# Storing one tile of a fused matmul in nine row pieces, and the tiles after it in six transfers

## The chip, the cores and the metric

One core of a Trainium2 chip. The metric is the device time of one execution in microseconds (us). Most executions of one kernel agree within 0.3%. Ratios are the mean time of one kernel's runs over that of the other's of the same rounds on the same chip, so they are not quite the ratio of the medians that are quoted; brackets give a 95% interval. A difference of 2% is the line for "faster" or "slower".

## The reference

```python
x: [16, 512, 1024] f32   weight: [1024, 768] f32   bias: [768]   residual: [16, 512, 768] f32
return (np.matmul(x, weight) + bias + residual).astype(np.float32)
```

The 8192 rows are worked in 64 tiles of 128 rows. 25.2 MB are written and 61.9 MB read.

## The kernel before

Each tile is cast to bf16, transposed and multiplied on TensorE (PE), and added to its residual on VectorE. All loads and stores are issued by SyncE (its queue is "SPq" in the profile), strictly in the order of one list, each, as the code reads, as soon as what it needs is finished (`# ...` marks what is cut; the comments are mine):

```python
ORDER = [ # ... kind, group S of 16 tiles, first and last tile in it, cuts in the 128 rows
 ('r', 3, 7, 16), ('s', 2, 0, 16), ('s', 3, 0, 10), ('s', 3, 10, 11, 104), ('s', 3, 11, 13),
 ('s', 3, 13, 14), ('s', 3, 14, 15), ('c', 3, 15, 0), ('c', 3, 15, 1)]
# ...
    def pump():
        while queue:
            kind, S, j0, j1, *cut = queue[0]
            # ...
            else:
                need = [("out", J * S + j) for j in range(j0, j1)]
            if not all(n in done for n in need):
                return                      # the head of the list holds up all the rest
            queue.pop(0)
            # ...
                edges = [0, *cut, P]
                for p0, p1 in zip(edges, edges[1:]):
                    K_(nc.sync.dma_start(
                        out=out_d[S, p0:p1, j0:j1, n0:n0 + nl],
                        in_=R[p0:p1, (J * S + j0) % RR:(J * S + j0) % RR + j1 - j0, n0:n0 + nl],
                    ))
```

So `('s', 2, 0, 16)` stores tiles 32 to 47 in one transfer, `('s', 3, 0, 10)` tiles 48 to 57, and `('s', 3, 10, 11, 104)` tile 58 as 104 and 24 rows. The semaphore (a counter that tells when all of a transfer has landed, that is, been written) is not in the code: the framework gives it out.

Of the kernel before, what the change touches and what calls it, by code (L numbers as in the profile page):

```python
# [32 lines left out]
 ('r', 0, 6, 16), ('x', 0, 14, 16), ('x', 1, 0, 6), ('r', 1, 0, 6), ('x', 1, 6, 16),  # L33
 ('r', 1, 6, 16), ('s', 0, 0, 16), ('x', 2, 0, 6), ('r', 2, 0, 6), ('x', 2, 6, 16),
 ('r', 2, 6, 16), ('s', 1, 0, 16), ('x', 3, 0, 6), ('r', 3, 0, 7), ('x', 3, 6, 16),
 ('r', 3, 7, 16), ('s', 2, 0, 16), ('s', 3, 0, 10), ('s', 3, 10, 11, 104), ('s', 3, 11, 13),
 ('s', 3, 13, 14), ('s', 3, 14, 15), ('c', 3, 15, 0), ('c', 3, 15, 1)]
LAST = [(0, 512), (512, 256)]


# [256 lines left out]
```

## Time and profile before

| | before |
|---|---|
| time, median | 210.32 us |
| span of the profiled run (that run took 210.12 us) | 208.3 us |
| PE busy | 201.8 us, 97% |
| DMA, 16 engines, main queue | 98.1% |
| last compute instruction ends | 204.5 us |
| last store issued, landed | 204.54, 207.25 us |

Both PE and DMA are nearly always busy.

### The profile page before, as it was taken

To read this page: it belongs to the slowest core of one execution; us is meant where nothing else is said; L and a number is where in the kernel's file an instruction comes from. 1 tells how busy PE (TensorE), PEld (TensorE's weight loads), DVE (VectorE), ACT (ScalarE), POOL (GpSimd) and SP (SyncE) were. 2 spreads that over 40 slices of the span, in tenths; PEclk is the share of its full clock that TensorE was granted. 3 is DMA by queue.
4 is the path that set the end of the run, shared out by engine and by line. 5 is a ranking of instruction groups with operands and counts; after the bars stand their busy time and mean duration, and the time that the engine had idled before them with its cause. 6 is when DMAs were issued, how large, how long until landed. Compare 5 with 4: busy or idle time off the path is not lost.

```text
span 208.3 us, 3115 instructions
## 1 busy us (share of the span) xinstructions
PE 201.8 (97%) x1298; PEld 130.1 (62%) x1298; DVE 104.7 (50%) x140; ACT 66.1 (32%) x69; POOL 116.0 (56%) x72
## 2 busy tenths in 40 slices
PE   7899999999999999999999999999999999999991
PEld 2455666666666666666666666666666666666651
DVE  0457555445545544654554454555445545544542
ACT  2444513403640272420370094230092046430000
POOL 2100029759999905999029702999207950599500
PEclk9999999999999999999999999999999999999998
DMA  6999999999989999999999999999999999999995
GB/s 233 427 429 436 424 432 457 388 446 421 495 383 466 405 423 427 434 426 415 425 465 418 422 436 452 415 437 406 434 446 451 409 419 475 428 396 444 416 368 221
DMA packets 4927, 87.24 MB, mean 419 GB/s; under 512 B 557, under 2 KB 685, under 8 KB 1841
## 3 DMA queue, kind: packets, MB, share of 16 engines
q1 hardware_dynamic: 4913, 87.05, 98.1%
q8 instruction: 10, 0.16, 0.3%
q14 instruction: 4, 0.03, 0.0%
HBM read 61.88 MB, written 25.17 MB: 418 GB/s over the span
## 4 chain that ended last, share of the span: by engine, by line
PE 92%; DMA 4%; DVE 1%; SPq 0%; ACT 0%; issue 0%
PE psum_o L164 78%; PE pt L157 13%; DMA x_tile<-in_x_dram 4%; PE psum_o L258 1%; DVE xt L158 0%; ACT xb L146 0%; DVE ro L262 0%; SPq L119 0%; SPq L122 0%
## 5 line engine op out<-in xcount | busy, mean ns | idle before, releaser
L164 PE MATMUL psum_o<-w_sb,xt 128*128 128x512 bf16 x1008 | 174.0, 326 | 0.5 <-DVE xt L158 0.3
L164 PEld LDWEIGHTS <-xt 128*128 128x128 bf16 x1008 | 98.5, 98 | 59.2 <-DVE xt L158 0.7
L189 POOL TENSOR_TENSOR ro<-ro,bias_sb 128x768 f32<-128x768 f32 x50 | 88.9, 1823 | 48.2 <-DMA ro<-in_residual_dram 37.7
L149 ACT CAST xb<-x_tile 128x1024 bf16<-128x1024 f32 x60 | 59.7, 1043 | 113.9 <-DMA x_tile<-in_x_dram 74.1
L158 DVE COPY xt<-pt 128x1024 bf16<-128x1024 bf16 x64 | 44.1, 691 | 84.4 <-PE pt L157 84.4
L199 DVE TENSOR_TENSOR ro<-psum_o,ro 128x768 f32<-128x768 f32 x49 | 46.5, 948 | 4.6 <-POOL ro L189 3.4
L185 POOL TENSOR_TENSOR ro<-ro 128x768 f32<-128x768 f32 x14 | 25.0, 1820 | 25.0 <-DMA ro<-in_residual_dram 25.0
L157 PE MATMUL pt<-ident,xb 128*128 128x128 f32 x256 | 38.3, 273 | 0.6 <-DVE xb L149 0.4
L157 PEld LDWEIGHTS pt<-ident,xb 128*128 128x128 f32 x256 | 29.7, 140 | 9.0 <-ACT xb L146 1.1
L195 DVE TENSOR_TENSOR ro<-psum_o,bias_sb 128x768 f32<-128x768 f32 x14 | 13.2, 947 | 0.0
L208 PE MATMUL psum_o<-warm 128*128 128x512 bf16 x12 | 4.8, 587 | 1.2 <-DVE warm_a L204 1.2
L229 ACT CAST w_sb<-ro 128x768 bf16<-128x768 f32 x4 | 3.3, 832 | 3.7 <-DMA ro<-in_weight_dram 3.7
L208 PEld LDWEIGHTS <-warm 128*128 128x128 bf16 x12 | 1.6, 141 | 3.9 <-issue 2.7
L229 POOL CAST w_sb<-ro 128x768 bf16<-128x768 f32 x1 | 0.8, 824 | 5.5 <-DMA ro<-in_weight_dram 5.5
L149 DVE CAST xb<-x_tile 128x1024 bf16<-128x1024 f32 x1 | 0.7, 694 | 4.5 <-DMA x_tile<-in_x_dram 4.5
L146 ACT CAST xb<-x_tile 128x512 bf16<-128x512 f32 x3 | 1.8, 617 | 3.4 <-PE psum_o L164 1.7
L258 PE MATMUL psum_o<-w_sb,xt 128*128 128x512 bf16 (+1 forms) x16 | 2.8, 326 | 0.0
L229 DVE CAST w_sb<-ro 128x768 bf16<-128x768 f32 x3 | 1.7, 556 | 2.0 <-DMA ro<-in_weight_dram 2.0
L147 DVE CAST xb<-x_tile 128x512 bf16<-128x512 f32 x3 | 1.2, 424 | 2.6 <-DMA x_tile<-in_x_dram 2.6
L258 PEld LDWEIGHTS <-xt 128*128 128x128 bf16 x16 | 1.6, 98 | 1.1
L223 PE MATMUL psum_o<-warm 128*128 128x512 bf16 x6 | 1.6, 379 | 0.0
L262 DVE TENSOR_TENSOR ro<-psum_o,ro 128x512 f32<-128x512 f32 (+1 forms) x2 | 1.1, 557 | 0.9 <-PE psum_o L258 0.8
(14 smaller groups left out, 5.1 us busy)
## 6 DMA issues: line engine op xcount, KB each, us to landing
out_dram<-ro SPq DMA_DIRECT2D x3, 6144.0 KB, 34.1
x_tile<-in_x_dram SPq DMA_DIRECT2D x3, 5120.0 KB, 24.1
ro<-in_residual_dram SPq DMA_DIRECT2D x3, 3840.0 KB, 25.3
x_tile<-in_x_dram SPq DMA_DIRECT2D x3, 3072.0 KB, 40.2
ro<-in_residual_dram SPq DMA_DIRECT2D x3, 2304.0 KB, 17.5
x_tile<-in_x_dram SPq DMA_DIRECT2D x4, 1024.0 KB, 8.3
x_tile<-in_x_dram SPq DMA_DIRECT2D x2, 2048.0 KB, 21.0
out_dram<-ro SPq DMA_DIRECT2D x1, 3840.0 KB
```

The costliest lines, as they stand in the source:

```text
L146: K_(nc.scalar.copy(out=dst[:, 0:K // 2], in_=src[:, 0:K // 2]))
L149: K_((nc.scalar.copy if how == "s" else nc.vector.tensor_copy)(out=dst, in_=src))
L157: K_(nc.tensor.transpose(out=pt[:, q, :], in_=words[:, ts(q, P)], identity=ident))
L158: K_(nc.vector.tensor_copy(out=XT[t % XT_N].rearrange("p q m e -> p (q m e)"), in_=pt.rearrange("p q m -> p (q m)").bitcast(BF16),))
L164: K_(nc.tensor.matmul(PO[t % HEAD][:, n0:n0 + nl], lhsT=XT[t % XT_N][:, q, :, e], rhs=w_sb[:, q, e, n0:n0 + nl], start=(q == 0 and e == 0) ...
L185: K_(nc.gpsimd.tensor_add(out=r, in0=r, in1=tmp(t)))
L189: K_(nc.gpsimd.tensor_add(out=r, in0=r, in1=bias_sb))
L195: K_(nc.vector.tensor_add(out=tmp(t), in0=p, in1=bias_sb))
L199: K_(nc.vector.tensor_add(out=row(t), in0=p, in1=row(t)))
L208: K_(nc.tensor.matmul(PO[0][:, 0:512], lhsT=warm[:, 0:P], rhs=warm, start=True, stop=True))
L229: K_(copy(out=w_sb[:, q, e, :], in_=w_st[:, 2 * q + e, :]))
L258: K_(nc.tensor.matmul(p, lhsT=XT[t % XT_N][:, q, :, e], rhs=w_sb[:, q, e, n0:n0 + nl], start=(q == 0 and e == 0), stop=(q == n_q - 1 and e ...
```

## The change

The intent is balance. The 16 DMA engines don't end together (the parts of the last store land from 206.18 to 207.25 us), and a transfer of few rows goes to some of the engines only: the prediction says to which, and from which page that is. The change gives tile 48 to the engines unevenly, and tile 58 evenly, together with 59 and 60:

```diff
- ('r', 3, 7, 16), ('s', 2, 0, 16), ('s', 3, 0, 10), ('s', 3, 10, 11, 104), ('s', 3, 11, 13),
- ('s', 3, 13, 14), ('s', 3, 14, 15), ('c', 3, 15, 0), ('c', 3, 15, 1)]
+ ('r', 3, 7, 16), ('s', 2, 0, 16), ('s', 3, 0, 1, 8, 15, 21, 26, 30, 33, 35, 126),
+ ('s', 3, 1, 10), ('s', 3, 10, 13), ('s', 3, 13, 14), ('s', 3, 14, 15), ('c', 3, 15, 0),
+ ('c', 3, 15, 1)]
```

## The prediction

> **What bounds the kernel now.** I read the page first, then the windows, then the DMA queue's own timeline and waits, and last the single packet and landing records of the trace.
>
> The page offers two candidates: PE is busy 97% of the span, the main DMA queue 98.1%.
>
> ```profile
> PE 201.8 (97%) x1298; PEld 130.1 (62%) x1298; DVE 104.7 (50%) x140; ACT 66.1 (32%) x69; POOL 116.0 (56%) x72
> ...
> q1 hardware_dynamic: 4913, 87.05, 98.1%
> q8 instruction: 10, 0.16, 0.3%
> ```
>
> Both run nearly without a gap, so the end decides. The windows (columns: busy us and count of each engine, then PE clock, DMA share, GB/s) show it:
>
> ```profile
> 180.00:206.00 26.00, 24.05 (x158) 15.51 (x156) 12.96 (x17) 3.14 (x3) 15.35 (x9) 1.00 0.97 407
> ...
> 204.00:205.00 1.00, 0.05 (x1) 0.00 (x0) 0.42 (x1) 0.00 (x0) 0.00 (x0) 1.00 0.87 350
> 205.00:206.00 1.00, 0.00 (x0) 0.00 (x0) 0.00 (x0) 0.00 (x0) 0.00 (x0) 1.00 0.97 368
> 206.00:207.00 1.00, 0.00 (x0) 0.00 (x0) 0.00 (x0) 0.00 (x0) 0.00 (x0) 0.91 0.28 99
> ```
>
> Compute is over at 204.5 us, and DMA still works at 0.97 until 206. The last store (256 columns of tile 63) is issued at 204.54. Its sixteen landing records lie between 206.18 and 207.25; the span ends at 208.3. The engines with no backlog needed 1.64 us (206.18 - 204.54); the slowest were 1.1 us late. So the DMA engines, not PE, set the end, and only by that 1.1 us. But they have no slack: any time in which they stand empty in the last 20 us is added to the end almost whole, because all of tiles 48 to 63 (6.29 MB) has still to be stored.
>
> The DMA queue's timeline at the end (start us, duration us):
>
> ```profile
> 157.96 0.34 SPq L130 DMA_DIRECT2D out_dram<-ro  x1
> ...
> 188.32 0.34 SPq L130 DMA_DIRECT2D out_dram<-ro  x1
> ...
> 191.36 1.64 SPq L130 DMA_DIRECT2D out_dram<-ro  x2
> ...
> 197.44 0.36 SPq L130 DMA_DIRECT2D out_dram<-ro  x1
> ```
>
> At 157.96 tiles 32 to 47 go out; at 188.32 tiles 48 to 57, the moment tile 57 is finished; then 58 in two, 59 and 60, and the rest. The first of these takes long to land, as the issues in 157 to 160 us show (KB, us to landing):
>
> ```profile
> out_dram<-ro SPq DMA_DIRECT2D x1, 6144.0 KB, 35.6
> ```
>
> 157.96 + 35.6 = 193.5. Its sixteen parts land one by one from 189.98 to 193.53; the rings go on with tiles 48 to 57 without a gap, because those were queued at 188.32, five microseconds before that last landing.
>
> One more thing bounds issues. The trace names the semaphore of each DMA, and the 36 of them go strictly round eight: 101, 104, 105, 106, 107, 108, 109, 110, 101 and so on. A DMA waits for the earlier one of its semaphore to land wholly. The ninth (x rows 6 to 9) and the tenth (residual) need no data of anyone, yet wait, as the queue's waits in 4.5 to 8 us say:
>
> ```profile
> SPq L124 <- DMA ro<-in_weight_dram: 1.5, 1, 1.5
> SPq L122 <- DMA x_tile<-in_x_dram: 0.6, 1, 0.6
> ```
>
> They start at 5.60 and 7.48; the first and second DMA landed at 5.58 and 7.47. At the end of before the rule costs nothing: the last eight stores use 107 to 106, and the last waits (at 204.39) for semaphore 106, which is that of tiles 32 to 47 and landed at 193.53.
>
> **What the Trainium skill says.** "DMA: Bandwidth & Descriptors", section "Why a DMA increments its semaphore by 16 and not by 1", says that a transfer is cut over the largest k up to 16 that divides its rows, on the lowest-numbered engines, and that only the full count means landed. The trace agrees: with k = 13 for 104 rows and 12 for 24, the packets I expect are exactly the 4913 of the page. So 8, 7, 6, 5, 4, 3, 2, 91 and 2 rows go to 8, 7, 6, 5, 4, 3, 2, 13 and 2 engines. The page's "Rules for kernel authors" ask for one semaphore per DMA; here eight are shared and guarded by waits. "Runtime: NRT & Kernel Launch", section "Instruction fetch mechanics", says instructions come in 16 KiB blocks: the 10 packets of q8 are these, some 19.5 us apart, at 177.13 and 196.13 last. It calls them mostly hidden for the sequencer; for a DMA engine they are not: the two engines hit last finish tiles 48 to 57 at 202.56 and 202.59, the next at 201.22, and eight 30,720-byte packets with a fetch took 10.57 us instead of 9.08, so 1.49 us each.
>
> **The change part by part.** The intent reads plainly: engines 0 and 1 get 15 rows of tile 48, falling to 7 for engines 8 to 12 and none for 13 to 15, and tile 58 goes back to 8 each. Per engine against before (18 rows for 0 to 11, 16 for 12, 8 for 13 to 15) that is +5 rows for engines 0 and 1, -3 for 8 to 11, 0 for 13 to 15. A row of 3072 bytes took 0.12 us, so this shifts at most 0.6 us. The two latest engines in before sent no packet of tile 58, so they are among 13 to 15 and gain nothing. From balance I expect 0.
>
> The issues are the larger matter. The S=3 stores become 15, numbers 28 to 42 counted from 0, with semaphores 107, 108, 109, 110, 101, 104, 105, 106, 107, 108 and so on. Tile 48 is ready at about 188.3 - 9 x 3.04 = 160.9 us.
> - Numbers 28 to 32 (8 to 4 rows): predecessors landed by 157.2; issued at once.
> - 33 (3 rows, 104): waits for the x load that landed at 169.34.
> - 34 (2 rows, 105): waits for the residual that landed at 179.23.
> - 35 (91 rows, 106): its predecessor is the store of tiles 32 to 47, so it waits until 193.53.
> - 37 (tiles 49 to 57), ready at 188.3, stands behind it in the same queue.
>
> So the issue of 3.5 MB moves from 188.32 to: 193.55, plus 0.41 for the 91 rows, plus 0.4 to 1.25 for the 2 rows (0.35 and 1.24 are the two short issues of before), so 194.4 to 195.2. From issue to first packet the last two stores took 0.83 and 0.95 us; I take 0.9 to 1.1. The engines, which ran out of tiles 32 to 47 between 189.5 and 193.1, restart on tiles 49 to 57 at 195.3 to 196.3.
>
> From there nothing waits for compute any more, and an engine needs, with the packet steps of before (bytes: us) 27,648: 1.024; 3072: 0.118; 2048: 0.081; 1024: 0.043, and 9216: 0.345 between 6144 and 16,384:
> 8 x 1.024 = 8.20; 8 x 0.345 = 2.76; two tiles of 8 x 0.118 = 1.88; 0.65; 0.34; in all 13.86 us with the small closing packets. Landing came 0.37 us after the last packet. An undisturbed engine lands at 195.8 + 13.86 + 0.37 = 210.0, that is 2.8 us later than 207.25.
>
> The engine that gets PE's fetch at 196.1 has 1.0 to 1.5 us more. PE's instructions don't change, so the fetch comes at the same time, now on an engine that has no spared tile ahead of it. Landing 211.0 to 211.7: +3.8 to +4.5 us. The other parts (seven more issues, their waits, one transfer for 58 to 60 at the same 197.44) lie beside this. With the middle, +4.0: 210.32 + 4.0 = 214.3.
>
> **The rivals.** (1) Balance works and nothing else happens: 209.6 to 210.4. For it speaks the 1.1 us of lateness; against it that the latest engines are not relieved, and the round of eight. (2) The stores of tile 48 fill time while the others wait, the restart is early and the fetch costs only 0.5 us: landing at 195.4 + 13.86 + 0.37 + 0.5 = 210.1, so 213.2. (3) Short transfers are slow to issue: if each of the two that stand before number 37 takes 1.24 us, it is issued at 196.1, restarts the engines at 197.1, lands at 211.3 without the fetch, and the time is 214.4 to 215.2. (4) PE as the bound: no store of the end is awaited by compute, so PE should not move.
>
> **Range and chances.** If the wait for semaphore 106 appears, 212.9 to 215.2 covers the spread of issue cost and fetch; I give that nine chances in ten. The 2% line is 214.53, inside this range and just above my middle, so slower by over 2% is nearly even. Nothing can make it faster by 2%, which would be 4.2 us of at most 0.7 to be had.
>
> **What would show it.** In the profile of after: the queue's waits should have an L130 entry for its own stores' DMA, with the 91-row store and that of tiles 49 to 57 issued after 193.5; DMA share near 0 around 194; PE's end unchanged at 204.1; the final wait of the queue (2.4 us before) some 4 us longer. I am wrong if tiles 49 to 57 are issued at 188.3 again: then the semaphores are given out otherwise, and rival 1 holds.

## More of the kernel before

What counts is the tail of the span: after the last compute instruction only stores are left. The prediction shows the lines for this; three windows that it doesn't show are needed later (columns: stretch in us, its length, busy us and number of instructions of PE, PEld, DVE, ACT and POOL, clock granted to PE, DMA share, GB/s):

```profile
190.00:192.00 2.00, 2.00 (x14) 1.18 (x13) 1.33 (x2) 0.00 (x0) 2.00 (x3) 1.00 0.74 316
192.00:194.00 2.00, 2.00 (x16) 1.40 (x14) 1.18 (x2) 0.00 (x0) 2.00 (x2) 1.00 1.03 445
194.00:196.00 2.00, 2.00 (x16) 1.36 (x15) 0.52 (x2) 0.00 (x0) 1.35 (x1) 1.00 0.96 415
```

A packet is counted in the stretch in which it starts, so single windows swing; the last two say that the engines were full between 192 and 196 us.

## The result, and the profile after

213.44 us (213.44 and 213.45 in two runs) against 210.32: ratio 1.0148 [1.0105, 1.0192]. It is slower by 1.5%, under the 2% line and inside the range. A second visit gave 213.53 against 210.61, ratio 1.0134 [1.0120, 1.0148].

The page of after (part 1, then the main queue of part 3) shows the same work, in 211.4 us:

```profile
PE 202.4 (96%) x1298; PEld 130.2 (62%) x1298; DVE 104.6 (49%) x140; ACT 66.1 (31%) x69; POOL 115.9 (55%) x72
...
q1 hardware_dynamic: 4938, 87.05, 96.8%
```

There are 25 more DMA packets for the same 87.05 MB, and a share that fell by 1.3 points. The windows say when it fell:

```profile
190.00:192.00 2.00, 2.00 (x14) 1.17 (x12) 1.32 (x2) 0.00 (x0) 2.00 (x2) 1.00 0.24 97
192.00:194.00 2.00, 2.00 (x16) 1.41 (x14) 1.20 (x2) 0.00 (x0) 2.00 (x2) 1.00 0.05 8
194.00:196.00 2.00, 2.00 (x16) 1.35 (x15) 0.52 (x2) 0.00 (x0) 1.24 (x1) 1.00 0.93 335
```

Between 192 and 194 us the engines moved 8 GB/s where they had moved 445, while PE worked as before; the 8 are one fetched block of PE's instructions (16 KiB, at 193.03), and no row of a store was begun. The queue's timeline tells why (start us, duration us):

```profile
157.80 0.34 SPq L131 DMA_DIRECT2D out_dram<-ro  x1
...
160.84 1.67 SPq L131 DMA_DIRECT2D out_dram<-ro  x5
...
193.67 0.31 SPq L131 DMA_DIRECT2D out_dram<-ro  x1
...
194.03 0.26 SPq L131 DMA_DIRECT2D out_dram<-ro  x1
...
194.38 0.36 SPq L131 DMA_DIRECT2D out_dram<-ro  x1
```

Five pieces of tile 48 go out at once, the sixth and seventh at 169.67 and 179.13. Then the queue stops: the piece of 91 rows is issued at 193.67, the last two rows at 194.03, and tiles 49 to 57 only at 194.38, where before had issued tiles 48 to 57 at 188.32. What it waited for, in 185 us to the end (us in total, times, longest):

```profile
SPq L131 <- DMA out_dram<-ro: 14.3, 1, 14.3
...
SPq L293 <- DMA out_dram<-ro: 4.7, 1, 4.7
```

The first line is the new one: 14.3 us for an earlier store. In the trace's instruction record, the 91-row issue waits on semaphore 106, which it also takes itself; that is the semaphore of the store of tiles 32 to 47, whose last landing record is at 193.65, 0.02 us before the issue. The second line is the wait at the kernel's end, 2.4 us in before. The chain of work still ends in the same place, as its last piece shows in before and after in turn (start us, us):

```profile
204.09 0.42 DVE ro L262
```

```profile
204.08 0.42 DVE ro L263
```

So compute did not move at all. The last landing did, from 207.25 to 210.34 us, 3.09 us later, and this is the whole loss (210.32 to 213.44 is 3.12).

### The profile page after: what moved, and what is told of

It reads as the page before. It is cut to its first block, busy times and chain, and to the rows that moved or that the text cites. A ratio compares the mean times of both kernels' runs of the same rounds, so it can differ in the third digit from the quotient of the medians.

```text
span 211.4 us, 3125 instructions
## 1 busy us (share of the span) xinstructions
PE 202.4 (96%) x1298; PEld 130.2 (62%) x1298; DVE 104.6 (49%) x140; ACT 66.1 (31%) x69; POOL 115.9 (55%) x72
## 3 DMA queue, kind: packets, MB, share of 16 engines
q1 hardware_dynamic: 4938, 87.05, 96.8%
## 4 chain that ended last, share of the span: by engine, by line
PE 91%; DMA 4%; DVE 1%; SPq 0%; ACT 0%; issue 0%
PE psum_o L165 77%; PE pt L158 13%; DMA x_tile<-in_x_dram 4%; PE psum_o L259 1%; DVE xt L159 0%; ACT xb L147 0%; DVE ro L263 0%; SPq L120 0%; SPq L123 0%
## 5 line engine op out<-in xcount | busy, mean ns | idle before, releaser
L209 PE MATMUL psum_o<-warm 128*128 128x512 bf16 x12 | 5.3, 632 | 1.2 <-DVE warm_a L205 1.2
L224 PE MATMUL psum_o<-warm 128*128 128x512 bf16 x6 | 1.6, 379 | 0.0
```

The source lines that it names most:

```text
L209: K_(nc.tensor.matmul(PO[0][:, 0:512], lhsT=warm[:, 0:P], rhs=warm, start=True, stop=True))
```

## The experiments

The theory: eight semaphores are given out in turn, and each transfer waits for the landing of the one eight before it. Nine pieces put the 91-row piece eighth after the long store of tiles 32 to 47, and tiles 49 to 57 stand behind it in an ordered queue. The rivals: that uneven rows on few engines, or the number of issues (15 instead of 8), or moving tile 48 ahead, cost the time themselves.

### Six pieces

```diff
-('s', 3, 0, 1, 8, 15, 21, 26, 30, 33, 35, 126)
+('s', 3, 0, 1, 8, 15, 21, 26, 37)
```

> Tile 48 in six transfers (8, 7, 6, 5, 11, 91 rows) instead of nine, all else as in the changed kernel. Theory (the eighth transfer after the store of tiles 32 to 47 takes its semaphore and waits for its landing): the eighth is now the store of tiles 58 to 60, which isn't ready before 197.4, so tiles 49 to 57 are issued at 188.3 and nothing is lost: 210.2 to 210.6 us. Rival A (uneven rows, or transfers on fewer than 16 engines, cost the time themselves): rows are about as uneven as in the changed kernel, 212.5 to 213.5. Rival B (each further issue costs): a proportional part, 212.2. Last instruction fetch of PE: near 196 as in the kernel before, since the DMA engines stay busy.

Measured: 210.82 us against 210.53, ratio 1.0012 [0.9996, 1.0029]. The median is 0.22 us above the expected band; the bands of these runs were worked out from 210.32 for the kernel before, which itself took 0.21 more here. The ratio is that of an equal. Tiles 49 to 57 went out as soon as they were ready:

```profile
188.77 0.35 SPq L131 DMA_DIRECT2D out_dram<-ro  x1
```

The queue still waited once for an earlier store, for 5.3 us, but now with the store of tiles 58 to 60, which was then not ready before 197.9 anyway. PE's last instruction fetch began at 197.84 us.

### Seven pieces

```diff
-('s', 3, 0, 1, 8, 15, 21, 26, 30, 33, 35, 126)
+('s', 3, 0, 1, 8, 15, 21, 26, 30, 37)
```

> Tile 48 in seven transfers (8, 7, 6, 5, 4, 7, 91 rows), one more than in the run of six. Theory: the eighth transfer is the store of tiles 49 to 57 itself; it is issued at about 193.7 instead of 188.3, first packets 194.6 to 194.7, then 13.86 us of packets and 0.37 to land: 208.9, so 211.8 to 212.3 us, a step of about 1.6 us between six and seven. Rivals A and B: within 0.4 us of the run of six. Last instruction fetch of PE: near 193, as its engine stands empty then.

Measured: 212.55 us, ratio 1.0097 [1.0082, 1.0112] with the same runs of before: a step of 1.7 us for one more piece, as the theory asks and no rival does. Tiles 49 to 57 are now themselves the eighth:

```profile
194.06 0.36 SPq L131 DMA_DIRECT2D out_dram<-ro  x1
```

The store of tiles 32 to 47 had landed at 194.00. The time lies 0.25 us above the expected band. The landing that it waited for came 0.35 us later in this run than in the one that the number was worked out from; the last store landed at 209.52, 0.6 us after the 208.9 worked out, so this is a part of it only.

### Eight even pieces

```diff
-('s', 3, 0, 1, 8, 15, 21, 26, 30, 33, 35, 126)
+('s', 3, 0, 1, 16, 32, 48, 64, 80, 96, 112)
```

> Tile 48 in eight transfers of 16 rows, each on all 16 engines, one row each: even, no transfer on fewer engines. Theory: the eighth transfer (16 rows) waits for the landing at 193.6, tiles 49 to 57 follow at about 194.05, first packets at 195.0: 212.2 to 212.8 us. Rival A: nothing uneven is left, so no more than the run with tile 48 in one transfer (211.3). Rival B: near the changed kernel, 213.

Measured: 213.09 us, ratio 1.0122 [1.0107, 1.0137]. The rows were wholly even and the loss was there, so unevenness is not its cause. (That each issue costs, rival B, would give this time too; the runs of six and seven, and the reordered one below, speak against it.) It is 0.3 us over the band, in part for the same reason: the landing was at 194.12, the eighth piece was issued at 194.14, and tiles 49 to 57 at 194.55.

### Tile 48 in one piece

```diff
-('s', 3, 0, 1, 8, 15, 21, 26, 30, 33, 35, 126)
+('s', 3, 0, 1)
```

> Tile 48 in one transfer of 128 rows, ahead of tiles 49 to 57 as in the changed kernel, tiles 58 to 60 together as there. Theory: no wait; but the two engines that end last in the kernel before, among the three that it spared 8 rows of tile 58, get these rows back, 8 x 0.118 = 0.94 us: 211.1 to 211.4 us. If moving tile 48 ahead, or merging 58 to 60, cost the time of the change: 213 or more. If sparing engines is worth nothing: 210.3.

Measured: 211.51 us, ratio 1.0045 [1.0030, 1.0060]; 0.98 us over before, against 0.94 worked out (the median is 0.11 above the band). So moving tile 48 ahead and merging tile 58 with its neighbours seem to cost nothing else. Two engines landed the last store at 208.58 and 208.66, all others by 207.24: this fits two engines that have their eight rows back, though no record names them. It is then what the trick with tile 58 in the kernel before is worth: cut into 104 and 24 rows, the tile spares three engines.

### The large piece first

```diff
-('s', 3, 0, 1, 8, 15, 21, 26, 30, 33, 35, 126)
+('s', 3, 0, 1, 91, 99, 106, 112, 117, 121, 124, 126)
```

> The nine transfers of the change with the one of 91 rows first, so that the eighth and ninth are of 2 rows. Theory: it doesn't matter what waits, only that tiles 49 to 57 stand behind it: they are issued at 194.4 again; the engines restart on them directly, without 91 rows ahead, at 195.4: 212.5 to 213.0 us. Rival (the late 91 rows, 273 KB, are what is lost): they are out by 192, so 210.5 to 211.2 us.

Measured: 213.03 us, ratio 1.0116 [1.0103, 1.0129], 0.03 us over the band. Here only two rows waited for the semaphore (issued at 193.98), and the loss is nearly the same. What waits doesn't matter; what stands behind it does.

### The nine transfers in another order

The cleanest test: the same fifteen stores with the same rows, but tiles 49 to 57 ahead of three small pieces. Kind `p` stores some rows of one tile.

```diff
- ('s', 2, 0, 16), ('s', 3, 0, 1, 8, 15, 21, 26, 30, 33, 35, 126), ('s', 3, 1, 10), ('s', 3, 10, 13),
+ ('s', 2, 0, 16), ('p', 3, 0, 0, 8), ('p', 3, 0, 8, 15), ('p', 3, 0, 15, 21),
+ ('p', 3, 0, 21, 26), ('p', 3, 0, 26, 30), ('p', 3, 0, 35, 126), ('s', 3, 1, 10),
+ ('p', 3, 0, 30, 33), ('p', 3, 0, 33, 35), ('p', 3, 0, 126, 128), ('s', 3, 10, 13),
```

> The same fifteen stores with the same rows as in the changed kernel; only the order of issue differs: 8, 7, 6, 5, 4 and 91 rows of tile 48, then tiles 49 to 57, and only then the 3, 2 and 2 rows. Theory: the eighth transfer after the store of tiles 32 to 47 is now that of 3 rows; it waits until about 193.6 as before, but tiles 49 to 57 are already queued at 188.3 to 188.8, so the engines have work and the time is that of the run with six transfers: 210.4 to 210.9 us. If the nine transfers, their rows or their number cost anything of themselves: 212.5 to 213.5. Last instruction fetch of PE: again near 196 to 198.

> The changed kernel once more, on the same chip, for comparison with the reordered one: 213.4 us (213.1 to 213.7), ratio to the kernel before 1.013 to 1.015; tiles 49 to 57 issued at 194.4; last instruction fetch of PE at about 193, on an engine that stands empty.

Measured side by side on one chip: reordered 210.83 us, ratio 1.0006 [0.9992, 1.0020]; the changed kernel again 213.53 us, ratio 1.0134. The order alone gives the 2.7 us back. The timeline of the reordered kernel:

```profile
188.24 0.35 SPq L141 DMA_DIRECT2D out_dram<-ro  x1
...
193.89 2.44 SPq L118 DMA_DIRECT2D out_dram<-ro  x3
```

The first line is tiles 49 to 57, the second the three small pieces. These still wait for the same landing (193.87 here), as the queue's waits after 185 us say:

```profile
SPq L118 <- DMA out_dram<-ro: 5.3, 1, 5.3
```

and the windows show that the engines don't notice:

```profile
192.00:194.00 2.00, 2.00 (x15) 1.40 (x14) 1.27 (x2) 0.00 (x0) 2.00 (x2) 1.00 1.11 475
```

A wait that stands behind the work costs nothing; the same wait ahead of it costs 2.7 us.

### The aim of the change, without the wait

```diff
-('s', 3, 0, 1, 8, 15, 21, 26, 30, 33, 35, 126), ('s', 3, 1, 10), ('s', 3, 10, 13),
+('s', 3, 0, 1, 19, 123), ('s', 3, 1, 10), ('s', 3, 10, 11, 96, 122), ('s', 3, 11, 13),
```

> What the change aims at, within seven transfers: tile 48 as 19, 104 and 5 rows (28, 9 and 8 rows on engines 0, 1 to 4 and 5 to 12, none on 13 to 15), tile 58 as 96, 26 and 6. The store after these is not due before 197.4, when semaphore 106 is free. The latest engines of the kernel before get 6 rows instead of 8, the engine late by 18 rows keeps 18: 0.24 us less at most, 210.1 us (209.9 to 210.3). If the lateness of single engines doesn't matter: 210.3. If waits come back: over 211.

Measured: 212.67 us (211.78 to 213.51 in six runs), ratio 1.0099 [1.0079, 1.0118]. This was a plain miss. No wait for a store held up the queue; tiles 49 to 57 were issued on time:

```profile
188.16 0.36 SPq L131 DMA_DIRECT2D out_dram<-ro  x1
```

In the traced run one engine landed its rows of the 104-row piece at 194.68, all others by 193.32, and stayed behind to the end: the last store landed at 209.49 on one engine and by 208.20 on the others. It is the engine that got the 19 rows: these landed at 192.95, and the eight rows that it had next, at 0.12 us each, can't have landed before 193.9. They took 1.73 us, 0.22 each; why, is not shown (the other engines were moving large packets by then).

The expectation gave this engine 28 rows of tile 48 and never added them up. With 9 rows of tile 58 it carries 37, where the kernel before gives no engine more than 18 of these two tiles: 19 x 0.118 = 2.2 us more. The last landing came 2.24 us later than in before (209.49 against 207.25). So the sum of rows alone forewarned of the miss; that it fits so closely may be luck, as it isn't known how much time this engine had to spare. Why the six runs differ by 1.7 us stays open. I know of no version that beats the kernel before: six pieces and the reordered nine equal it.

## Why the prediction was right or wrong

**The bound.** Right. PE ended where it had, and what was added is empty time of the DMA engines in the tail.

**The waits of numbers 28 to 37.** Right in each item: issues at 160.84 to 162.5 for the first five, 169.67 for 33 (predicted 169.34), 179.13 for 34 (179.23), 193.67 for 35 (193.55), 194.38 for tiles 49 to 57 (194.4 to 195.2, missed by 0.02). The six and seven pieces and the reordered nine show that this is the cause, not only beside it.

**The issue of the short pieces.** The 91 and the 2 rows took 0.31 and 0.26 us to issue, steps of 0.36 and 0.35 us to the next issue where 0.41 and 0.4 to 1.25 had been put in: just under the low end. Rival 3, 1.24 us each, fell.

**Restart and drain.** The engines' first packets of tiles 49 to 57 started between 195.43 and 196.18 us (predicted 195.3 to 196.3). The engine that started last should have landed at 196.18 + 13.86 + 0.37 = 210.41; the last landing was at 210.34.

**PE's fetch at 196.1.** This step failed. I had said that the fetch comes at the same time, on an engine with no spared tile ahead of it, and adds 1.0 to 1.5 us. It came at 193.03 instead, into the empty stretch, and added nothing visible: the sixteen landings of the last store lie between 209.75 and 210.34 with no straggler. This is the term that made 214.3 out of a kernel that takes 213.4; without it the sum was 2.8 us, against 3.1 measured. That sum had taken the restart of an engine in the middle, 195.8; with the 196.18 of the last one it is 3.16.

Five traces with the empty stretch have the last fetch at 193.0 to 193.4 us, and five without it (before, six, one, reordered, balanced) at 196.1 to 197.8, though PE ran alike (its end differs by 0.6 us at most). So the fetch is likely asked for at about 193 in all of them, and served three to five us later where its engine has packets to move. I had taken the time at which it was served for the time at which it was asked for. That no run shows the request itself leaves this an inference, though a consistent one.

Three smaller figures were wrong too. Followed through the trace by their times, the eight packets with a fetch took 10.47 us and not 10.57, so 1.4 us more and not 1.49. The fetches lie 19.2 us apart in the mean, not 19.5. And 1.0 to 1.5 us on top of 210.0 end at 211.5, not at 211.7.

**Balance.** I expected 0, as the two latest engines keep their load. The run with six pieces, which has nearly the same rows and no stall, was at 1.0012, and the reordered nine, with exactly the same rows, at 1.0006: that agrees. The run with tile 48 in one piece measured the trick of before at 0.98 us against 0.94 for 8 rows x 0.118. My own attempt at balance failed by the same arithmetic, which I had not done for the engine with 19 rows.

**The signs.** All came but one in size: the final wait of the queue was to be some 4 us longer and is 2.3 longer (4.7 against 2.4). The end is 3.09 us later, but the last store took 1.10 us to issue instead of 0.33, and the wait begins after that.

**The page on semaphores.** The Trainium skill, "DMA: Bandwidth & Descriptors", section "Why a DMA increments its semaphore by 16 and not by 1", counts a transfer as landed only at its full count, that is at its slowest engine. Here this was expensive: fifteen of the sixteen parts of the store of tiles 32 to 47 had landed by 192.38 us, and the queue waited for the sixteenth until 193.65.

## What to carry to other kernels

Count the transfers. Where completion semaphores are reused in turn, each issue waits for the landing of the transfer that many places before it, and in an ordered queue everything behind waits too; cutting a small store into pieces can therefore hold up a large one that has nothing to do with it. With eight semaphores here, the next large transfer was free as the seventh after the long one (six pieces between) and held up as the eighth (seven pieces between). So keep it fewer places behind than there are semaphores, or put the small pieces behind the large one, which here cost nothing.

## What the Trainium skill lacked or had wrong

- "DMA: Bandwidth & Descriptors", section "Rules for kernel authors", asks for a dedicated semaphore but does not tell what reuse costs: here 2.7 us of 213.5, recovered by order alone (213.53 against 210.83).
- "Runtime: NRT & Kernel Launch", section "Instruction fetch mechanics", calls the cost of crossing a block mostly hidden, which is said of the sequencer; it doesn't tell what a fetch costs a saturated DMA engine. Here 16 KiB took 0.9 to 1.1 us of it, and in before eight packets with a fetch took 1.4 us more than without. Nor does it tell when a fetch is served: the last one began at 193.0 to 193.4 us with empty engines, at 196.1 to 197.8 with full ones.
- "DMA: Bandwidth & Descriptors", section "Specifications", gives 512 bytes as the least transfer for line rate; being over it was not enough here. 3072-byte packets usually took 0.121 us, but up to 0.349 in the 91-row piece after the restart, 0.476 in the run of the aimed balance and 0.489 in before.
- The same page, section "Issuing engines are not separate DMA queues", calls the time of issue usually small beside the DMA itself. One store of 2 rows took 0.26 us to issue in the changed kernel and 1.04 in the reordered one, and the last store 0.33 in before and 1.10 in after. No page I read says what this depends on, and no run here settles it.
